# Norm sums taken in the row passes, squares on ScalarE, late features on two engines, the T1 product first, and attention memory in parts: one decoder layer on one core

## The chip, the core and the metric

The kernel runs on one core of a Trainium2 chip. The metric is the device time of the program in microseconds; it was run three times, and the number compared is the median. TensorE (PE, with its weight loads PEld) multiplies, VectorE (DVE), ScalarE (ACT) and GpSimd (POOL) work on rows in SBUF, and SyncE (SP) issues nearly all DMA transfers from one queue in program order.

## The reference

One layer of a decoder for 1024 prompt rows and 8 x 8 = 64 sample rows, width 1024. A mixer (one half sliding-window attention, the other a spatial gating unit) and a feed-forward part, each with an adaptive modulation ahead and a norm behind:

```python
h = layer_norm(x) * (1 + scale1) + shift1
q, k, v, zu, zv = split(h @ w_in)
A = attention(rotary(q), rotary(k), v, sinks)      # 8 heads, 2 key heads, window 128
B = gelu(zu) * (tril(w_s) @ layer_norm(gelu(zv)) + b_s)
x = layer_norm(ALPHA * x + gate1 * concat(A, B) @ w_o, ln1_g, ln1_b)
h = layer_norm(x) * (1 + scale2) + shift2
x = layer_norm(ALPHA * x + gate2 * (silu(h @ w_gate) * (h @ w_up)) @ w_down, ln2_g, ln2_b)
...
var = mean((xf - mu)**2);  y = (xf - mu) * rsqrt(var + LN_EPS) * gain + bias
```

shift, scale and gate come from silu(c) @ w_ada + b_ada. All is float32. The feed-forward width is 2816. The rolled key and value windows and the normalised v rows are outputs too.

## The kernel before

Every matrix product is made from fp32 numbers split into a high part that TensorE takes (ScalarE copies it) and a low rest (VectorE subtracts); three products (high-high, high-low, low-high) are summed in PSUM. A weight unit is loaded by SP, split by `load_unit` (L104 ScalarE, L105 VectorE) or `w_split` (L956, L957), and used. The order on each engine is set by a scheduler that runs a timeline model over the program as it is written; a pool's buffer (and the memory under a pool that was closed) can be written only when its last reader is done, and the scheduler puts the waits in. PSUM has four tags, a to d, of two banks each.

The stages, with their time in the profiled run:

- **Conditioning, first projections and the gating unit** (0 to about 172 us). x is normalised in six tiles that use the memory `xb`; features go to XA and XB (three column chunks of 384, 384 and 320). Later in the stage `xb` holds the rotary tables rc and rs, the sample keys and values KC and VC, the masks, the cleared sample queries QZ and an output buffer o2s. `L414` is VectorE's pass that ends the gating unit, `L408` its products.
- **Attention** (to about 350). `project` (L496) multiplies one 128-row weight unit with the features; `rotate` shuffles the result (L505, VectorE) into `sh`, copies it (L506, ScalarE) into `z`, and rotates on POOL. Keys (units[0]) come in three chunks c, then values (units[1]) with a copy `v32`, then queries. `attend` makes scores (masked by L596), softmax (L614), the transposes of the weights (L643) and the products with the values (L651), and writes into one tile `stash` of 4 x 1024 columns. At the end `split_attention` (L449, L450) splits the stash, tile by tile, into the memory of the features.
- **Output projection and first norm** (350 to about 450). `load_wo` splits eight weight units; four go to a pool `w3`, in the memory that the attention's pools leave. `out_group(2)` multiplies tiles 6, 7 and 8 (L212), `out_tile` the tiles 0 to 5. `merge_tile` scales the sums by the gate (L838, one per half); `norm_tile` adds x, takes the statistics by `ln_stats` (two bn_stats L115, one aggregation, one add on VectorE, a power on POOL L121), applies gain and bias (L855 and the pass behind it), stores the row, takes the statistics again and normalises on ScalarE (L134). Tiles 6 and 7 (`PRE`) were multiplied in part before, and add on POOL. `ffn_features` transposes the normed tiles (L880), modulates them on ScalarE (L901), and stores every block of features to DRAM (`h_d`); prompt tiles of the first 512 places also stay in XA, split.
- **Feed-forward, gate and up** (450 to 960). The products over pairs of 128-row blocks are made by a seven-product scheme over quarters of the features: B11 and B21 (first 512 places) lie in SBUF, T1 to T4 and B22 are sums and differences of quarters read back from `h_d` into `hb` (L1089, `part`), combined on VectorE (L961) and split. `gu_head(0)` and `gu_head(1)` work with B11 and B21 alone (L967, sample part L973); `gu_p5` takes T1, `gu_p6` T2, `gu_p3` B22, `gu_p7` T3, `gu_p4` T4. `gated` stores the result to `g_d`; `copied` is the tile j.
- **Down projection and last norm** (960 to the end).

The places on which the two weight passes of a pair's head, the reads of `h_d` and the writes of `h_d` meet are the SP queue and VectorE: both run in their program's order, whoever waits first. The code of the T stage is written so: heads 0 and 1; then T1 from eight reads, one statement for `gu_s1` of both pairs (L1100), then B22 and T2 to T4 from sixteen reads, then `gu_22` and `sample_down`, and only then `gu_p5` of both pairs.

## Time and profile before

| | us |
|---|---|
| three runs | 1190.87, 1191.7, 1192.7; median 1191.7 |
| the profiled execution | 1190.98, its span 1189.2 |
| mean granted TensorE clock in it | 0.979 |
| POOL busy | 171.1 (14%) |
| HBM read, written | 149.43 MB, 55.44 MB |

Busy times are sums over the span, in which stages with different limits follow one another. The rows of the slices give busy tenths and the clock that TensorE was granted; a slice below 9 on PE is a place where it waited. The profile's share of the chain that ended last is 76% PE and 10% DVE. A group of the profile (line, engine, operation, out<-in) has its busy time, the mean of one instruction in ns, and the idle time ahead of it with its releaser.

### The profile page before, as it was taken

Reading aid. Unit: us, or ns where it says so; the run is one execution under the profiler, and the core shown is the slowest. Engines: PE = TensorE matmul, PEld = TensorE weight load, DVE = VectorE, ACT = ScalarE, POOL = GpSimd, SP = SyncE. Lnnn points to the kernel's source line nnn. Section 1 sums busy time; section 2 is a strip of 40 time slices with the busy share of each in tenths; the row PEclk is TensorE's granted clock in tenths of the full one; section 3 lists DMA queues with packets and bytes.
Section 4 is the critical chain, followed back from the end, with each engine's and each line's share of the span. In section 5 each row is a group of like instructions: output and inputs, shape, how many; then the busy total and the mean of one; then the engine's idle time right before and its main releaser. Section 6 shows DMA issues by size and latency. Waiting matters only on the chain.

```text
span 1189.2 us, 16244 instructions
## 1 busy us (share of the span) xinstructions
PE 1126.9 (95%) x5845; PEld 914.7 (77%) x5845; DVE 801.2 (67%) x1460; ACT 505.3 (42%) x920; POOL 171.1 (14%) x173
## 2 busy tenths in 40 slices
PE   4999998999979999799999999999999999999997
PEld 2676688887758877477888888888888888788885
DVE  4434355898776979568487467467467565879786
ACT  3553124675761255545444434434433454343200
POOL 2212434654135111000000000000000000000021
PEclk9999998999989999799999999999999999999999
DMA  9935344122353424554545515515514488957951
GB/s 330 296 109 188 96 148 154 56 76 94 107 194 119 152 100 168 181 175 139 202 161 195 203 47 193 204 54 186 203 52 170 151 313 290 336 193 258 325 204 71
DMA packets 96352, 204.96 MB, mean 172 GB/s; under 512 B 10304, under 2 KB 32704, under 8 KB 96256
## 3 DMA queue, kind: packets, MB, share of 16 engines
q1 hardware_dynamic: 96272, 203.92, 49.6%
q8 instruction: 46, 0.75, 0.3%
q14 instruction: 34, 0.28, 0.1%
HBM read 149.43 MB, written 55.44 MB: 172 GB/s over the span
## 4 chain that ended last, share of the span: by engine, by line
PE 76%; DVE 10%; DMA 7%; ACT 3%; issue 2%; SPq 1%; POOL 1%; DVEq 0%; ACTq 0%; POOLq 0%
PE ps_a L967 17%; PE ps_b L967 13%; PE ps_a L212 11%; PE ps_b L212 4%; PE ps_c L973 3%; PE ps_a L1243 3%; PE ps_b L1243 3%; PE ps_c L1243 3%; PE ps_d L1243 3%; DMA g<-g_d 2%; PE ps_a L496 2%; DMA rwd<-in_w_down 1%; PE ps_d L364 1%; DVE s L614 1%; DVE bn L115 1%
## 5 line engine op out<-in xcount | busy, mean ns | idle before, releaser
L967 PE MATMUL ps_a<-H,wgu 128*128 128x512 f32 x560 | 160.1, 390 | 1.3 <-ACT wgu L956 1.3
L967 PEld LDWEIGHTS ps_a<-H,wgu 128*128 128x128 f32 x560 | 105.1, 188 | 23.7 <-ACT wgu L956 1.7
L957 DVE TENSOR_TENSOR wgu<-rawgu,wgu 128x1024 fp32r<-128x1024 f32 x79 | 96.2, 1220 | 33.1 <-ACT wgu L956 33.0
L1280 POOL TENSOR_TENSOR rstd<-ve,neghalf 128x1 f32<-128x1 f32 (+1 forms) x9 | 13.6, 1513 | 695.1 <-DVE ve L1278 695.1
L212 PE MATMUL ps_a<-unit,XA 128*128 128x512 f32 x384 | 103.9, 413 | 6.5 <-ACT unit L104 4.7
L956 ACT ACTIVATE wgu<-rawgu 128x1024 fp32r<-128x1024 f32 x79 | 82.0, 1055 | 58.4 <-PE ps_a L967 48.0
L967 PE MATMUL ps_b<-H,wgu 128*128 128x512 f32 x320 | 104.1, 390 | 0.0
L967 PE MATMUL ps_b<-XA,wgu 128*128 128x512 f32 x344 | 96.6, 396 | 0.0
L212 PEld LDWEIGHTS ps_a<-unit,XA 128*128 128x128 f32 x384 | 73.2, 196 | 28.0 <-ACT unit L104 4.9
L873 DVE TENSOR_TENSOR tpo<-tpr,tpo 128x512 fp32r<-128x512 f32 x77 | 50.9, 686 | 60.6 <-ACT tpo L872 60.6
L967 PEld LDWEIGHTS ps_b<-XA,wgu 128*128 128x128 f32 x344 | 65.0, 191 | 13.2
L872 ACT ACTIVATE tpo<-tpr 128x512 fp32r<-128x512 f32 x77 | 45.1, 625 | 66.8 <-DMA tpr<-in_w_down 32.5
L967 PEld LDWEIGHTS ps_b<-H,wgu 128*128 128x128 f32 x320 | 60.0, 188 | 12.7 <-ACT H L872 0.5
L967 PE MATMUL ps_a<-XB,wgu 128*128 128x512 f32 x160 | 62.4, 390 | 0.0
L961 DVE TENSOR_TENSOR rawgu<-rawgu 128x1024 f32<-128x1024 f32 x44 | 53.3, 1211 | 12.4 <-DMA rawgu<-in_w_gu 12.4
L1243 PE MATMUL ps_a<-opnd 128*128 128x512 f32 x198 | 57.9, 391 | 3.2 <-ACT opnd L1220 3.2
L967 PE MATMUL ps_a<-XA,wgu 128*128 128x512 f32 x240 | 59.8, 392 | 0.0
L1243 PE MATMUL ps_b<-opnd 128*128 128x512 f32 x198 | 57.6, 389 | 0.0
L1243 PE MATMUL ps_c<-opnd 128*128 128x512 f32 x198 | 57.4, 389 | 0.0
L1243 PE MATMUL ps_d<-opnd 128*128 128x512 f32 x198 | 57.2, 389 | 0.0
L496 PE MATMUL ps_a<-XA,unit 128*128 128x384 f32 (+1 forms) x264 | 51.5, 342 | 4.8 <-ACT z L506 3.3
L967 PEld LDWEIGHTS ps_a<-XA,wgu 128*128 128x128 f32 x240 | 44.3, 188 | 8.8
(361 smaller groups left out, 2355.9 us busy)
## 6 DMA issues: line engine op xcount, KB each, us to landing
rawgu<-in_w_gu SPq DMA_DIRECT2D x44, 512.0 KB
t_d<-tpo SPq DMA_DIRECT2D x44, 512.0 KB
opnd<-t_d SPq DMA_DIRECT2D x33, 512.0 KB
tpr<-in_w_down SPq DMA_DIRECT2D x22, 512.0 KB
g<-g_d SPq DMA_DIRECT2D x44, 256.0 KB
u<-in_w_ada SPq DMA_DIRECT2D x32, 256.0 KB
raw<-in_w_ada SPq DMA_DIRECT2D x16, 512.0 KB
raw<-in_w_ada SPq DMA_DIRECT2D x32, 256.0 KB
```

What stands on the lines that cost most here:

```text
L115: nc.vector.bn_stats(out=bn[:rows, h, :], in_=src[:, 512 * h : 512 * (h + 1)])
L212: mm(out=pt, lhsT=X[c][:, xp, k, off : off + P], rhs=rhs_of(units, k, wp), start=st and q == 0, stop=sp and q == 2)
L496: mm(out=pt[:, :n], lhsT=w[:, wp, k * P : (k + 1) * P], rhs=X[c][:, xp, k, :], start=(k == 0 and q == 0), stop=(k == KD - 1 and q == 2))
L872: nc.scalar.activation(out=hi, in_=src, func=AF.Copy)
L873: nc.vector.tensor_tensor(out=lo, in0=src, in1=hi.bitcast(F32), op=ALU.subtract)
L956: nc.scalar.activation(out=w[:, 0], in_=r, func=AF.Copy)
L957: nc.vector.tensor_tensor(out=w[:, 1], in0=r, in1=w[:, 0].bitcast(F32), op=ALU.subtract)
L961: nc.vector.tensor_tensor(out=out, in0=in0, in1=in1, op=op)
L967: mm(out=banks[m], lhsT=w[:, wp, m, k * P : (k + 1) * P], rhs=b[xp][:, k, :], start=first and k == 0 and q == 0, stop=last and k == 3 and ...
L973: mm(out=pt[:, 256 * half : 256 * half + 256], lhsT=XF[:, k0 + k, :], rhs=w[:, wp, :, k * P : (k + 1) * P], start=first and k == 0 and wp ...
L1243: mm(out=banks[tb], lhsT=st[sp][:, tb * P : (tb + 1) * P], rhs=mv[wp], start=first and q == 0, stop=last and q == 2, skip_group_check=True)
L1280: nc.gpsimd.tensor_tensor(out=rstd[:rows], in0=ve[:rows], in1=neghalf[:rows], op=ALU.pow)
```

## The change

It has five parts.

1. **Early key temporaries.** `xb` is cut into `xb` (5 x 1024 columns) and a pool `xc` of its own that holds QZ and o2s. The shuffle and copy of key chunks 0 and 1 (`sh`, `z`) no longer take buffers of `rt`, but the memory of KC and VC, and the first two `v32` that of o2s and QZ. So the loads of KC and VC move from the gating stage behind the key chunks, and the clearing of QZ (POOL) behind the value chunks. `sh` gets a pool of its own.
2. **Attention memory in parts.** `stash` becomes four tiles in four pools (two query tiles each), and the pool of the output weights, `w3`, four pools of one buffer.
3. **Norm statistics.** In `norm_tile` the bn_stats go. The row sum comes out of the passes that run anyway (`accum_out` of the add, and of the gain and bias pass), a small VectorE pass makes the mean, a ScalarE pass squares the centred row and sums it (its row output goes to `xt`, which so is held longer), another small one makes the variance, and POOL takes the power. PRE tiles add on VectorE instead of POOL. `h32` has 4 buffers instead of 6.
4. **Late features.** The features of the last tiles (tiles 3, 4 and 5, as `normed[6:8]` and `normed[8:9]`; they are places 5 to 7 and so lie in the second 512) are made by `late_features`: four transposes into one bank, the modulation of every other block on VectorE instead of ScalarE, and one DMA for a bank: 6 writes instead of 16.
5. **T1 product in front.** `gu_head(1)` loads two weight blocks instead of four; behind T1 come `gu_s1(0)` and at once the T1 product of pair 0, then the other two blocks of pair 1, `gu_s1(1)`, `gu_22` and `sample_down` of both pairs, and behind them B22 and T2 to T4. The T1 product of pair 1 stays where it was. `sample_down` transposes into its own sample bank instead of bank b.

The core of the diff:

```diff
+    xc = xcp.tile([P, D], F32, name="xc")
+    xb = xbp.tile([P, 5 * D], F32, name="xb")
...
+    QZ, o2s = xc[:, 0:512], xc[:, 512:1024]
+    early = [t[:, o : o + 384] for t in (KC, VC) for o in (0, 512)] + [o2s[:, 0:384], QZ[:, 0:384]]
...
-        nc.sync.dma_start(out=KC, in_=kc_t)
-        nc.sync.dma_start(out=VC, in_=vc_t)
...
-    stash = stp.tile([P, 4, SEQ], F32, name="stash")
+    for n in (3, 0, 1, 2):
+        stp = st_ctx.enter_context(tc.tile_pool(name=f"stash{n}", bufs=1, side="right", reuse_waits="tile"))
+        stash[n] = stp.tile([P, 4, 2 * P], F32, name=f"stash{n}")
...
-            sh = rt.tile([P, 384], F32, tag="sh", name="sh")
-            z = rt.tile([P, 384], F32, tag="z", name="z")
+            sh, z = own or [q.tile([P, 384], F32, tag=g, name=g) for q, g in ((shp, "sh"), (rt, "z"))]
...
-            z = rotate(project(units[0], c, "aac"[c]), c)
+            z = rotate(project(units[0], c, "aac"[c]), c, early[2 * c : 2 * c + 2] if c < 2 else None)
...
+        nc.sync.dma_start(out=KC, in_=kc_t)
+        nc.sync.dma_start(out=VC, in_=vc_t)
...
-            v32 = rt.tile([P, 384], F32, tag="z", name="v32")
+            v32 = early[4 + c] if c < 2 else rt.tile([P, 384], F32, tag="z", name="v32")
...
+        nc.gpsimd.memset(QZ, 0.0)
...
-        w3 = w3_ctx.enter_context(tc.tile_pool(name="w3", bufs=4, side="right", reuse_waits="tile"))
+        w3 = [
+            w3_ctx.enter_context(tc.tile_pool(name=f"w3{n}", bufs=1, side="right", reuse_waits="tile"))
+            for n in range(4)
+        ]
...
         def norm_tile(i, r, xt):
...
+            def spread(o):
+                nc.vector.tensor_scalar(
+                    out=st[:, o + 1 : o + 2], in0=st[:, o : o + 1], scalar1=-1.0 / D, scalar2=None, op0=ALU.mult
+                )
+                nc.scalar.activation(
+                    out=xt[:rows], in_=rr, func=AF.Square, bias=st[:, o + 1 : o + 2], accum_out=st[:, o + 2 : o + 3]
+                )
...
+                nc.gpsimd.tensor_tensor(out=rstd[:rows], in0=st[:, o + 3 : o + 4], in1=neghalf[:rows], op=ALU.pow)
+                return st[:, o + 1 : o + 2], rstd[:rows]
...
-            mv, rstd = ln_stats(rr, D, rows)
             nc.vector.scalar_tensor_tensor(
-                out=rr, in0=rr, scalar=mv[:rows, 0:1], in1=lg[:rows], op0=ALU.subtract, op1=ALU.mult
+                out=rr, in0=xt[:rows], scalar=1.0 if i in PRE else ALPHA, in1=rr, op0=ALU.mult, op1=ALU.add,
+                accum_out=st[:, 0:1],
             )
+            nm, rstd = spread(0)
+            nc.vector.scalar_tensor_tensor(out=rr, in0=rr, scalar=nm, in1=lg[:rows], op0=ALU.add, op1=ALU.mult)
             nc.vector.scalar_tensor_tensor(
-                out=rr, in0=rr, scalar=rstd[:rows, 0:1], in1=lb[:rows], op0=ALU.mult, op1=ALU.add
+                out=rr, in0=rr, scalar=rstd, in1=lb[:rows], op0=ALU.mult, op1=ALU.add, accum_out=st[:, 4:5]
             )
...
+        def late_features(xn):
+            w = P * len(xn)
+            kb = 512 // w
+            o = P * PLACE[xn[0][0]]
+            for k0 in range(0, KD, kb):
...
+                for kk in range(kb):
+                    cs = slice(w * kk, w * kk + w)
+                    sc_, sh_ = scale_of(mod2, k0 + kk)[:, 0:1], shift_of(mod2, k0 + kk)[:, 0:1]
+                    if kk % 2:
+                        nc.vector.tensor_scalar(
+                            out=h[:, cs], in0=pt[:, cs], scalar1=sc_, scalar2=sh_, op0=ALU.mult, op1=ALU.add
+                        )
+                    else:
+                        nc.scalar.activation(out=h[:, cs], in_=pt[:, cs], func=AF.Identity, scale=sc_, bias=sh_)
+                nc.sync.dma_start(
+                    out=h_d[k0 : k0 + kb, :, o : o + w].rearrange("k p t -> p k t"),
+                    in_=h.rearrange("p (k t) -> p k t", k=kb),
+                )
...
-        rs = w_raws(p)
+        rs = w_raws(p, range(2) if p == 1 else range(4))
...
-        pt = bank("b" if p < 2 else "d")
+        pt = sp if p < 2 else bank("d")
...
-        w1 = [gu_s1(p, rs, sp) for p, (rs, sa, sp) in enumerate(heads)]
+        w1 = [gu_s1(0, heads[0][0], heads[0][2])]
+        p5 = [gu_p5(0, heads[0][0], w1[0], "b")]
+        heads[1][0].extend(w_raws(1, range(2, 4)))
+        w1.append(gu_s1(1, heads[1][0], heads[1][2]))
+        for p, (rs, sa, sp) in enumerate(heads):
+            gu_22(p, rs, sp)
+            sample_down(p, sp)
...
-        p5 = [gu_p5(p, rs, w1[p], "bd"[p]) for p, rs, sa in two]
+        p5.append(gu_p5(1, heads[1][0], w1[1], "d"))
```

Where instructions stand is decided by the scheduler, so the two programs' order is shown at three places. First VectorE, where the gating unit ends and the keys begin; before (L414 is the gating pass, L505 the keys' shuffle out of PSUM, L105 a weight split):

```order
L394 TENSOR_TENSOR gvt<-g_1412,gvt 128x512
L414 SCALAR_TENSOR_TENSOR u_1_124<-ps_b,bst,u_1_124 128x4x64 x6
L105 TENSOR_TENSOR unit<-raw,unit 128x1024
L414 SCALAR_TENSOR_TENSOR u_1_124<-ps_b,bst,u_1_124 128x4x64 x2
L505 STREAM_SHUFFLE sh<-ps_a 128x384 x2
```

The same place on VectorE in the changed program (its lines are 2 to 3 higher; xb is the memory of KC and VC):

```order
L508 STREAM_SHUFFLE xb<-ps_a 128x384
L396 TENSOR_TENSOR gvt<-g_1414,gvt 128x512
L508 STREAM_SHUFFLE xb<-ps_a 128x384
L416 SCALAR_TENSOR_TENSOR u_1_128<-ps_b,bst,u_1_128 128x4x64 x4
L508 STREAM_SHUFFLE sh<-ps_c 128x320
L105 TENSOR_TENSOR unit<-raw,unit 128x1024
L416 SCALAR_TENSOR_TENSOR u_1_128<-ps_b,bst,u_1_128 128x4x64 x4
```

The two shuffles of bank a moved ahead of the eight last gating passes. The second place is TensorE at the end of the attention, before (L643 transposes, L651 products with the values, L212 the output projection):

```order
L643 MATMUL ps_c<-ident,s 128x128 x4
L651 MATMUL ps_d<-pT,VS 128x256 x5
L643 MATMUL ps_c<-ident,s 128x128 x4
L651 MATMUL ps_d<-pT,VS 128x256 x3
L643 MATMUL ps_c<-ident,s 128x128 x4
L651 MATMUL ps_d<-pT,VS 128x256 x8
L212 MATMUL ps_a<-unit,XA 128x512 x4
L212 MATMUL ps_b<-unit,XA 128x512 x4
```

And in the changed program (L649 and L657 are the transposes and the products with the values there):

```order
L649 MATMUL ps_c<-ident,s 128x128 x4
L212 MATMUL ps_a<-unit,XA 128x512 x2
L212 MATMUL ps_b<-unit,XA 128x512 x2
L657 MATMUL ps_d<-pT,VS 128x256
L212 MATMUL ps_a<-unit,XA 128x512 x10
L212 MATMUL ps_b<-unit,XA 128x512 x10
L657 MATMUL ps_d<-pT,VS 128x256 x4
L212 MATMUL ps_a<-unit,XA 128x512 x4
L212 MATMUL ps_b<-unit,XA 128x512
L649 MATMUL ps_c<-ident,s 128x128
L657 MATMUL ps_d<-pT,VS 128x256 x3
L649 MATMUL ps_c<-ident,s 128x128 x7
```

The first output products now stand between the last attention steps instead of behind them. The third place is the SP queue, where the last features are written and the reads for T1 begin, before (L906 writes features, L950 loads gate and up weights, L979 stores a gated tile):

```order
L906 DMA h_d<-h_4691 128x128
L906 DMA h_d<-h_4696 128x128
L950 DMA rawgu<-in_w_gu 128x1024 x2
L1089 DMA hb<-h_d 128x512 x6
L979 DMA g_d<-j_4891 128x512
L1089 DMA hb<-h_d 128x512 x2
```

And after (L961 writes late features, L1138 reads for the T sums, L999 loads weights, L1028 stores):

```order
L961 DMA h_d<-hl 128x2x256 x3
L1028 DMA g_d<-j_4736 128x512
L961 DMA h_d<-hl 128x2x256
L961 DMA h_d<-hl 128x4x128 x2
L1138 DMA hb<-h_d 128x512 x4
L999 DMA rawgu<-in_w_gu 128x1024 x2
L1138 DMA hb<-h_d 128x512
L1028 DMA g_d<-j_4824 128x512
L1138 DMA hb<-h_d 128x512 x7
```

Six wide writes stand for the sixteen narrow ones, the two weight loads moved from ahead of the reads to behind the first four, and no row is left between the last write and the first read.

55 lines of the change are left out of this document (30 added, 25 removed).

## The prediction

> **What bounds the kernel now.** I read the page's head first, then its slices, then three stretches where TensorE is not full, and there the waits and the timeline.
>
> ```profile
> span 1189.2 us, 16244 instructions
> PE 1126.9 (95%) x5845; PEld 914.7 (77%) x5845; DVE 801.2 (67%) x1460; ACT 505.3 (42%) x920; POOL 171.1 (14%) x173
> PE   4999998999979999799999999999999999999997
> PEclk9999998999989999799999999999999999999999
> ```
>
> TensorE bounds the kernel, and it is short of work only at the start, in slices 6, 11 and 16 (counted from 0, 29.7 us each) and at the end. From slice 17 to 38 it stays full, and the change hardly touches what runs there. So only these stretches can pay:
>
> ```profile
> 172.00:205.00 33.00, 28.21 (x163) 27.59 (x163) 17.57 (x36) 12.96 (x27) 10.56 (x11) 0.90 0.44 153
> 325.00:360.00 35.00, 25.63 (x189) 19.26 (x188) 24.02 (x62) 21.86 (x52) 14.62 (x11) 0.85 0.55 185
> 447.70:542.30 94.60, 81.50 (x342) 62.12 (x341) 67.85 (x104) 51.11 (x87) 4.82 (x5) 0.87 0.49 165
> ...
> PE ps_d L973 <- DVE wgu L957: 4.4, 3, 1.9
> PE ps_a L496 <- ACT z L506: 3.3, 1, 3.3
> ```
>
> The columns of a window are its length, busy time of PE, weight loads, DVE, ACT and POOL, the granted clock, and DMA. TensorE idles 4.8, 9.4 and 13.1 us in them, and runs at 0.85 to 0.90 of its clock: each gap is paid again in slow products after it. The last two rows are TensorE's waits (product and releaser: idle us, times, longest): few single waits are long, so the idle time is looked for row by row. A timeline row gives start, duration, engine, line and operation, and in brackets the wait and its releaser.
>
> **Part 1, early key temporaries.** The keys' second block was multiplied by 171.8, but its two readers come late, since their outputs lie in memory that the stage before still uses. Bank a (two buffers) stays full, and the values' first block waits for it.
>
> ```profile
> 167.51 4.32 PE L496 MATMUL ps_a<-XB,unit 128*128 128x384 f32 x24
> 179.93 0.58 DVE L505 STREAM_SHUFFLE sh<-ps_a 128x384 f32<-128x384 f32 x1
> 181.14 7.27 PE L496 MATMUL ps_a<-XA,unit 128*128 128x384 f32 x24 [3.27 <-ACT z L506]
> 188.25 4.33 PE L496 MATMUL ps_a<-XB,unit 128*128 128x384 f32 x24
> 194.10 2.61 PE L496 MATMUL ps_a<-XA,unit 128*128 128x320 f32 x16 [1.52 <-ACT v L548]
> ```
>
> It costs 3.27 idle, 7.27 - 4.33 = 2.94 of slow products, and 1.52 more: 7.7 us. The change puts these temporaries where the sample keys and values (KC, VC) would lie, and the order has the shuffles ahead of L414, so the bank is free about 174, before TensorE asks for it (181.14 - 3.27 = 177.9). What is late next is the query rotation on POOL; two more query blocks (the 4.33 above and a narrower one, some 8 us) lie between query block 0 and the first scores and cover it. KC and VC are loaded behind it: their issue waits on the SP queue for the key splits, with conditioning weights behind it, and nobody reads them before 320; I cost that at nothing (a late weight load could cost a wait of 1 to 3 us). The clearing of QZ joins POOL's queue between query rotations, about one 0.5 to 1 us pass. I take **7.5** of the 7.7. The lower end is 0: behind it DVE is nearly full, and could swallow the head start:
>
> ```profile
> 240.00:260.00 20.00, 19.52 (x140) 19.14 (x139) 19.73 (x67) 14.80 (x41) 11.53 (x13) 1.00 0.15 48
> ```
>
> **Part 2, attention memory in parts.** The first output weights (L104) wait until the last split of the one large stash is over, though the masks were last read at 334:
>
> ```profile
> 333.98 0.48 DVE L596 CUSTOM_DVE_ANT_0 s<-ps_b,xb,nsnk 128x256 f32<-128x256 f32 x1
> 350.32 2.00 ACT L104 ACTIVATE unit<-raw 128x1024 fp32r<-128x1024 f32 x2 [0.84 <-DVE XB L450]
> 351.43 2.08 PE L212 MATMUL ps_a<-unit,XA 128*128 128x512 f32 x4 [4.70 <-ACT unit L104]
> 353.30 1.67 PE L212 MATMUL ps_b<-unit,XA 128*128 128x512 f32 x4
> ...
> 335.00:340.00 5.00, 3.62 (x36) 2.53 (x36) 3.70 (x13) 2.90 (x9) 0.71 (x1) 0.75 0.85 205
> 340.00:345.00 5.00, 4.36 (x26) 3.46 (x26) 4.94 (x10) 4.27 (x8) 2.41 (x2) 0.91 0.47 178
> 345.00:350.00 5.00, 0.98 (x7) 0.58 (x5) 4.55 (x9) 3.20 (x6) 0.00 (x0) 0.77 0.37 105
> 350.00:355.00 5.00, 3.57 (x9) 2.61 (x10) 2.64 (x3) 2.95 (x3) 1.17 (x1) 0.54 0.99 383
> ```
>
> Idle: 1.38 + 0.64 + 4.02 + 1.43 = 7.5 us. The eight first products take 3.75 where 8 x 0.227 (24 in 5.44, below) is 1.8, so 1.9 more: 9.4. With parts, two weight splits stand right behind the last masked scores, and 36 of the 48 products of tiles 6 and 7 lie between the last attention steps. Their 8.2 us (x 0.227) fill the gaps; what is late next is the attention chain itself, which three weight splits on DVE (3 x 1.22) now delay, against DVE idle of 1.3 and 0.1 in the first two windows; some 1 us remains. I take **8.5**; the ends are 0 (another tile in the same memory still holds the weights) and 9.4.
>
> **Part 3, norms, late features, T1.** From the last output product (447.7) to 542.3 the same products stand in both programs: 240 of 512 columns, 64 of 256, 42 or less of 128.
>
> ```profile
> 466.88 7.08 PE ps_b L967 x24
> 542.30 5.68 PE ps_a L967 x24
> 547.99 5.44 PE ps_c L967 x24
> ...
> 449.41 1.59 PE L973 MATMUL ps_d<-wgu,XF 128*128 128x256 f32 x12
> 450.12 0.67 DVE L838 TENSOR_TENSOR r<-ps_b,g1p 128x512 f32<-128x512 f32 x1
> 475.29 0.55 POOL L121 TENSOR_TENSOR rstd<-ve,neghalf 128x1 f32<-128x1 f32 x1 [3.21 <-DVE ve L119]
> 477.26 1.23 ACT L134 ACTIVATE r<-r,nb,rstd 128x1024 f32<-128x1024 f32 x1
> 478.40 5.10 ACT L901 ACTIVATE h<-ps_c,mod 128x256 f32<-128x256 f32 x10
> 479.00 4.00 PE L880 MATMUL ps_c<-ident,r 128*128 128x128 f32 x8 [0.89 <-ACT h L901]
> 484.95 9.77 SPq L1089 DMA_DIRECT2D hb<-h_d  x6
> 491.34 0.69 DVE L961 TENSOR_TENSOR hb<-hb 128x512 f32<-128x512 f32 x1
> 501.97 0.50 PE L967 MATMUL ps_d<-H,wgu 128*128 128x512 f32 x1 [1.31 <-DVE ts L961]
> 505.41 5.93 SPq L1089 DMA_DIRECT2D hb<-h_d  x4
> ...
> L115 DVE BATCH_NORM_STATS2 bn<-r 128x6 f32<-128x512 f32 x32 | 20.0, 678 | 0.1
> L855 DVE SCALAR_TENSOR_TENSOR r<-r,mv,lg 128x1024 f32<-128x1024 f32 x8 | 10.2, 1278 | 0.0
> L134 ACT ACTIVATE r<-r,nb,rstd 128x1024 f32<-128x1024 f32 x8 | 9.9, 1242 | 16.1 <-DVE nb L131 16.1
> L957 DVE TENSOR_TENSOR wgu<-rawgu,wgu 128x1024 fp32r<-128x1024 f32 x5 | 6.1, 1221 | 1.2 <-ACT wgu L956 1.1
> ```
>
> At full speed they need 240 x 0.227 + 64 x 0.13 + about 4 = 67 us, so some 28 of 94.6 are lost. The last tile's sums leave PSUM at 450.8, and its transposes start at 479.0, since DVE is full.
>
> Removed: four L115 per tile, 2.7 us of DVE. Added: two squaring passes on ACT, at L134's 1.24 and a short read-out each. The nine tiles' 2.8 us each (25 us) lie beside products that fill TensorE; if ACT had no room, they would come out again in part. The sum in the pass that already runs is not in this trace: between 0 and another 1.28; I take 0 to 0.1, as a pass with two sources reads at one rate here.
>
> Walking DVE's new order from the last L838: about 6.2 us of other tiles' and weights' passes (1.28, 1.22, 2 x 1.2, 3 x 0.4 and small ones), the tile's first pass 1.2, two weight splits and a sum 3.65 (the square lies beside them), two norm passes 2.6, a sum 1.2, three splits 1.3: 16.2. Then square 1.4, POOL 0.6, normalization 1.24 and hand-overs of about 1.5: 21, so transposes near 472 instead of 479. The features that took ten ACT passes from 478.4 are shared by two engines and two writes. Behind the first half go head 1's 24 products (5.44, perhaps 7), so the second half is written near 481 and the T1 reads issue there, not at 484.95 behind two weight loads. By the issue row the before needed 3.5 to 6.4 us to the first use at 491.34 (the row's six issues begin at 484.95); T1's first operand stands near 488, and its product there instead of 501.97. Its last operands are paced by DMA and two weight loads ahead of them on SP; near 495 the T2 to T4 reads start, which stand at 505.41 now. That chain took 30 us, is not changed, and now ends the stage: with the second T1 product beside it, TensorE reaches the row of 542.30 some **12** us sooner. Ends: 0, if the last tile is normalized no sooner, and 20, if only 8 of 28 stay lost.
>
> **Sum.** 7.5 + 8.5 + 12 = 28. The profiled execution took 1191.0 in all (1189.2 and 1.8 around it), 0.7 below the median shown; 1191.0 - 28 = **1163 us**.
>
> **Rivals.**
> - **T1 first only moves the wait.** The T2 to T4 chain waits for the same two DVE and DMA queues as before, so only about 4 of the 12 remain: 1171. For it: that chain is behind T1 on the queues. Against: its first reads can issue some 10 us sooner.
> - **The attention pieces do not carry.** DVE at 19.73 of 20 swallows part 1, or the weights still wait as before: 1163 + 8 to 16 = 1171 to 1179. Against: DVE has 15.4 of 33 idle at the entrance.
> - **The summing pass costs double.** At 2 x 1.28 for 18 passes DVE gets 23 us, about what 36 L115 (24 us) give up. The middle stays hidden under TensorE, but the last two tiles are some 5 us later: 1168. [...]
> - **Slower: DVE waits in line for the square and for POOL.** Each statistic now crosses DVE, ACT, DVE, POOL, DVE. If nothing lay between, a tile would hold DVE 9 us of work and 2 x 3 to 4.5 of waits (square 1.24, POOL 0.55, hand-overs, at most the 3.21 of POOL's row), 15 to 18, where TensorE brings a tile every 11 us (48 x 0.227). Above 11 it decides: six tiles lose 4 to 7 each, up to 42, and with 28 - 12 gained the time is about 1215. Against: the order has other tiles' passes between nearly all of these pairs.
>
> **How the numbers follow.** Forecast 0.58, T1 0.16, attention 0.10, double sum 0.08, slower 0.08. Range: the ends of the terms do not fall together; 1150 is 28 and the upper ends of parts 2 and 3 plus a little on the clock, 1181 leaves 10 gained. By 0.2% (about 2 us, what a measurement of this kernel tells from no change) faster has 0.90 (of the attention and T1 cases 0.02 go to same), same 0.02, slower 0.08.
>
> **What would show it.** Right: no wait of the values' products for z; L212 between the last attention products, window 345 to 355 full at clock 1; transposes of the last tile some 21 us after its last sums; T1's product 13 us after that. Wrong: an accumulating pass near 2.5 us, DVE idle on ACT between 360 and 447 with TensorE below 20 of 20, or the T2 to T4 products still ending 90 us after the last output product.

## The result and the profile after

| | before | changed |
|---|---|---|
| median of six runs each (us) | 1192.2 (1190.87 to 1195.15) | 1183.53 (1182.93 to 1185.2) |
| ratio, with its 95% interval | 1 | 0.9928 (0.9914 to 0.9942) |
| profiled execution, its span (us) | 1190.98, 1189.2 | 1184.88, 1183.1 |

The change gains 8.7 us by the medians and 6.1 by the profiled spans. The forecast was 28, and 1183.53 lies 2.5 above the end of the range. First the slices of the changed kernel's page:

```profile
PE   4999999989989998799999999999999999999997
PEclk9999999998999999789999999999999999999999
```

Slice 6 is full now and slice 11 a little better, but slices 8 and 15 have lost work that they had, and slices 9 and 17 clock. To see what each stage gave, both traces are cut where TensorE has done the same product columns: entrance of the attention, its middle, its tail into the output projection, and the T stage. The windows of the kernel before, then of the changed one, with the columns of the prediction's windows:

```profile
176.39:223.62 47.23, 41.70 (x244) 40.61 (x243) 28.80 (x64) 22.22 (x51) 25.89 (x26) 0.93 0.32 109
223.62:314.05 90.43, 86.74 (x724) 73.68 (x723) 79.91 (x257) 62.59 (x179) 40.53 (x43) 0.98 0.29 92
314.05:371.60 57.55, 47.89 (x318) 37.80 (x317) 39.10 (x101) 32.49 (x80) 18.27 (x13) 0.91 0.46 154
447.20:561.23 114.03, 100.93 (x429) 78.26 (x428) 84.70 (x124) 59.46 (x98) 4.82 (x5) 0.90 0.50 170
```

```profile
176.81:216.21 39.40, 38.48 (x246) 37.95 (x246) 27.45 (x65) 23.94 (x57) 22.10 (x25) 1.00 0.45 158
216.21:313.02 96.81, 89.07 (x733) 75.07 (x732) 87.26 (x263) 61.50 (x176) 39.41 (x43) 0.96 0.28 91
313.02:365.50 52.48, 46.79 (x306) 36.99 (x305) 33.84 (x89) 29.81 (x73) 14.01 (x11) 0.93 0.47 159
441.96:554.31 112.35, 98.94 (x433) 78.58 (x432) 83.53 (x126) 62.77 (x103) 3.72 (x5) 0.89 0.53 180
```

The lengths differ by -7.8 at the entrance, **+6.4** in the middle, -5.1 in the tail and -1.7 in the T stage. The output projection between the last two (371.60 to 447.20, 365.50 to 441.96) is 0.9 longer, and what lies ahead and behind 1.2, which makes -6.1. The gain at the entrance came as forecast, and in these two executions most of it was handed back in the middle: TensorE idles 0.9 us instead of 5.5 at the entrance, but 7.7 instead of 3.7 in the middle. The T stage, which had the largest term, gave almost nothing; TensorE idles 13.4 us in it, where it idled 13.1. The 2.6 us between the medians' 8.7 and the profiles' 6.1 come from the two executions that were profiled: 1190.98 lies 1.2 below the median of the one kernel, 1184.88 lies 1.35 above that of the other.

**The entrance.** The changed kernel's windows over the two times that the prediction looked at:

```profile
172.00:205.00 33.00, 33.00 (x216) 32.87 (x215) 19.02 (x40) 15.97 (x32) 17.59 (x18) 1.00 0.53 185
...
240.00:260.00 20.00, 17.60 (x147) 15.52 (x145) 19.67 (x47) 12.80 (x33) 10.34 (x11) 1.00 0.09 26
```

172 to 205 is full at clock 1: no value product waits any more. But between 240 and 260, where TensorE had 19.52 of 20, it has 17.60, with VectorE as full as before (19.67): 47 passes now fill a time that 67 filled.

**The middle.** The same 36 softmax scalings stand in both middles. The groups of VectorE in that stage, first before, then changed:

```profile
L596 DVE CUSTOM_DVE_ANT_0 s<-ps_b,xb,nsnk 128x256 f32<-128x256 f32 x42 | 18.6, 474 | 0.6 <-PE ps_c L643 0.4
L614 DVE TENSOR_SCALAR s<-s,den 128x256 f32<-128x256 f32 x36 | 16.4, 509 | 0.1
```

```profile
L620 DVE TENSOR_SCALAR s<-s,den 128x256 f32<-128x256 f32 x36 | 21.5, 652 | 0.3
L602 DVE CUSTOM_DVE_ANT_0 s<-ps_b,xb,nsnk 128x256 f32<-128x256 f32 x42 | 18.6, 476 | 2.7 <-PE ps_c L649 2.5
```

The masked scores, which read PSUM, take 18.6 us in both. The scaling, which reads and writes SBUF, takes 5.1 us more for the same work. One step of each kind shows why; four scalings before (VectorE alone), then four in the changed kernel with what POOL does meanwhile:

```profile
235.25 1.13 DVE L614 TENSOR_SCALAR s<-s,den 128x256 f32<-128x256 f32 x4
```

```profile
248.25 3.49 DVE L620 TENSOR_SCALAR s<-s,den 128x256 f32<-128x256 f32 x4
248.47 1.02 POOL L109 TENSOR_TENSOR sh<-sh,xb 128x384 f32<-128x384 f32 x1
249.45 1.06 POOL L109 TENSOR_TENSOR z<-z,xb 128x384 f32<-128x384 f32 x1
250.59 1.00 POOL L109 TENSOR_TENSOR z<-z,sh 128x384 f32<-128x384 f32 x1
```

Four scalings take 1.13 us alone and 3.49 beside three passes of the query rotation: the first, begun 0.22 ahead of them, takes 0.35; the other three take 1.10 to 1.16 each and end 0.15 behind the ends of the three POOL passes (249.49, 250.51, 251.59). The four scalings ahead of the middle went the other way, from 3.96 to 2.60 us, so the whole program has 24.1 us of them instead of 20.3. Of the 40 scalings of the whole program 20 lay beside POOL before, 27 after. Why they last until POOL's passes end these rows do not show.

**The tail.** The changed kernel's timeline where its last attention products end:

```profile
353.24 2.08 PE L212 MATMUL ps_a<-unit,XA 128*128 128x512 f32 x4 [2.00 <-ACT unit L104]
355.11 1.71 PE L212 MATMUL ps_b<-unit,XA 128*128 128x512 f32 x4
```

Its windows there:

```profile
345.00:350.00 5.00, 5.00 (x31) 4.24 (x29) 2.93 (x7) 2.20 (x5) 0.00 (x0) 1.00 0.66 183
350.00:355.00 5.00, 3.00 (x13) 2.44 (x12) 4.76 (x9) 3.40 (x6) 0.00 (x0) 0.80 0.94 306
```

Output products fill 345 to 350 at full clock, where there were 0.98 of 5. But the fourth weight unit still comes only with the end of the attention: a wait of 2.0 instead of 4.7 us, with slow products behind it (the two rows, 2.08 and 1.71 us for eight) as before.

**The T stage.** The SP queue of the changed kernel from T1's reads to the last read, then T1's first product on TensorE (the first eight reads are T1's, the ninth begins at 492.17):

```profile
477.38 4.37 SPq L1138 DMA_DIRECT2D hb<-h_d  x4
...
492.17 6.89 SPq L1138 DMA_DIRECT2D hb<-h_d  x4
...
505.64 14.94 SPq L1138 DMA_DIRECT2D hb<-h_d  x9
522.84 2.31 SPq L1138 DMA_DIRECT2D hb<-h_d  x3
...
484.54 1.22 PE L1016 MATMUL ps_b<-H,wgu 128*128 128x512 f32 x2 [4.18 <-ACT H L896]
```

And the same queue before, with the first and the last of the sixteen reads for B22 and T2 to T4:

```profile
503.68 7.67 SPq L1089 DMA_DIRECT2D hb<-h_d  x5
...
524.37 9.29 SPq L1089 DMA_DIRECT2D hb<-h_d  x7
```

Counted from the start of the stage (447.20 and 441.96), T1's reads stand 35.4 behind it instead of 37.8, the first T2 to T4 read 50.2 instead of 56.5, the last one ends 83.2 behind instead of 86.5. The head start shrinks from 6.3 to 3.3 us, because the sixteen reads take 33.0 us instead of 30.0. VectorE shows what lies between (L1010 on hb is a T sum, which frees the reads' buffers; L1010 on rawgu and L1006 are weight passes):

```profile
494.56 0.68 DVE L1010 TENSOR_TENSOR hb<-hb 128x512 f32<-128x512 f32 x1
495.16 1.22 DVE L1010 TENSOR_TENSOR rawgu<-rawgu 128x1024 f32<-128x1024 f32 x1
496.30 1.22 DVE L1006 TENSOR_TENSOR wgu<-rawgu,wgu 128x1024 fp32r<-128x1024 f32 x1
...
498.64 1.21 DVE L1010 TENSOR_TENSOR rawgu<-rawgu 128x1024 f32<-128x1024 f32 x1
...
500.38 2.34 DVE L1006 TENSOR_TENSOR wgu<-rawgu,wgu 128x1024 fp32r<-128x1024 f32 x2
...
503.78 1.23 DVE L1006 TENSOR_TENSOR wgu<-rawgu,wgu 128x1024 fp32r<-128x1024 f32 x1
504.93 0.69 DVE L1010 TENSOR_TENSOR hb<-hb 128x512 f32<-128x512 f32 x1
```

Between the T sums at 494.56 and 504.93 VectorE does six weight passes, 7.2 us, and the read at 505.64 stands right behind the second of these sums. In the program before, `gu_22` and the sample parts stood behind the T sums; the change writes them ahead.

### The profile page after: what moved, and what is told of

Same layout as the page of the kernel before. It is cut to its first block, busy times and chain, and to the rows that moved or that the text cites. A ratio compares the mean times of both kernels' runs of the same rounds, so it can differ in the third digit from the quotient of the medians.

```text
span 1183.1 us, 16238 instructions
## 1 busy us (share of the span) xinstructions
PE 1122.4 (95%) x5845; PEld 912.2 (77%) x5845; DVE 790.8 (67%) x1452; ACT 521.8 (44%) x948; POOL 162.7 (14%) x171
## 4 chain that ended last, share of the span: by engine, by line
PE 62%; DMA 6%; DVE 3%; ACT 2%; issue 1%; SPq 1%; DVEq 0%; ACTq 0%
PE ps_a L1016 17%; PE ps_b L1016 14%; PE ps_a L212 4%; PE ps_b L212 3%; PE ps_c L1022 3%; PE ps_a L1295 3%; PE ps_b L1295 3%; PE ps_d L1295 3%; PE ps_c L1295 3%; DMA g<-g_d 2%; DMA rwd<-in_w_down 1%; PE ps_c L1016 1%; DMA rawgu<-in_w_gu 1%; PE ps_c L1200 1%; PE ps_d L1200 1%
## 5 line engine op out<-in xcount | busy, mean ns | idle before, releaser
L1006 DVE TENSOR_TENSOR wgu<-rawgu,wgu 128x1024 fp32r<-128x1024 f32 x79 | 96.0, 1220 | 31.6 <-ACT wgu L1005 31.1
L1016 PE MATMUL ps_b<-H,wgu 128*128 128x512 f32 x320 | 107.5, 402 | 7.0 <-ACT H L896 4.2
L1005 ACT ACTIVATE wgu<-rawgu 128x1024 fp32r<-128x1024 f32 x79 | 81.8, 1054 | 61.3 <-PE ps_a L1016 48.0
L212 PE MATMUL ps_a<-unit,XA 128*128 128x512 f32 x384 | 102.9, 410 | 3.1 <-ACT unit L104 2.0
L212 PEld LDWEIGHTS ps_a<-unit,XA 128*128 128x128 f32 x384 | 72.6, 195 | 24.2 <-issue 2.5
L1295 PE MATMUL ps_b<-opnd 128*128 128x512 f32 x198 | 57.6, 389 | 0.0
L1010 DVE TENSOR_TENSOR rawgu<-rawgu 128x1024 f32<-128x1024 f32 x44 | 53.4, 1213 | 3.3 <-DMA rawgu<-in_w_gu 3.2
L500 PE MATMUL ps_a<-XA,unit 128*128 128x384 f32 (+1 forms) x264 | 47.7, 325 | 0.0
```

The costliest lines, as they stand in the source:

```text
L212: mm(out=pt, lhsT=X[c][:, xp, k, off : off + P], rhs=rhs_of(units, k, wp), start=st and q == 0, stop=sp and q == 2)
L500: mm(out=pt[:, :n], lhsT=w[:, wp, k * P : (k + 1) * P], rhs=X[c][:, xp, k, :], start=(k == 0 and q == 0), stop=(k == KD - 1 and q == 2))
L1005: nc.scalar.activation(out=w[:, 0], in_=r, func=AF.Copy)
L1006: nc.vector.tensor_tensor(out=w[:, 1], in0=r, in1=w[:, 0].bitcast(F32), op=ALU.subtract)
L1010: nc.vector.tensor_tensor(out=out, in0=in0, in1=in1, op=op)
L1016: mm(out=banks[m], lhsT=w[:, wp, m, k * P : (k + 1) * P], rhs=b[xp][:, k, :], start=first and k == 0 and q == 0, stop=last and k == 3 and ...
```

## The experiments

Each kernel ran beside fresh runs of the kernel before on the same chip, and its ratio is to these. The changed kernel itself has 0.9928, and 0.9911 as a control on another chip, so differences of 0.002 in the ratio are not told apart. The stage lengths are those of windows cut as above, from one profiled execution each (us), and hold the slow clock as well as the idle time:

| kernel | median (runs) | ratio, 95% | entrance | middle | tail | T stage |
|---|---|---|---|---|---|---|
| before | 1192.2 (6) | 1 | 47.2 | 90.4 | 57.6 | 114.0 |
| changed | 1183.53 (6) | 0.9928 [0.9914, 0.9942] | 39.4 | 96.8 | 52.5 | 112.4 |
| changed, control | 1183.73 (6) | 0.9911 [0.9891, 0.9930] | 39.4 | 98.4 | 52.5 | 113.1 |
| part 1 and the pool of sh undone | 1191.8 (10) | 0.9971 [0.9958, 0.9984] | 50.3 | 90.4 | 57.0 | 111.9 |
| part 1 undone, pool kept | 1189.63 (9) | 0.9964 [0.9949, 0.9979] | 48.5 | 90.9 | 53.3 | 113.3 |
| part 3 undone | 1188.29 (6) | 0.9943 [0.9923, 0.9963] | 39.4 | 98.4 | 53.3 | 118.8 |
| part 4 undone | 1186.57 (6) | 0.9932 [0.9913, 0.9951] | 39.4 | 96.8 | 52.3 | 115.4 |
| part 5 undone | 1183.14 (5) | 0.9891 [0.9872, 0.9911] | 39.4 | 94.3 | 53.5 | 110.2 |
| before, with part 3's norm alone | 1194.48 (10) | 0.9995 [0.9978, 1.0013] | 47.9 | 90.3 | 59.1 | 113.1 |
| before, short POOL passes | 1187.0 (4) | 0.9937 [0.9914, 0.9960] | 47.7 | 89.1 | 56.8 | 111.0 |
| changed, short POOL passes | 1174.37 (4) | 0.9835 [0.9811, 0.9859] | 38.0 | 88.7 | 49.6 | 112.4 |
| pair 2's loads behind the reads | 1182.69 (6) | 0.9897 [0.9871, 0.9923] | 39.4 | 97.1 | 53.2 | 111.5 |
| pair 0 finished first | 1199.35 (11) | 1.0039 [1.0026, 1.0051] | 39.4 | 95.5 | 52.2 | 128.5 |
| weight passes behind the T splits | 1207.75 (4) | 1.0097 [1.0069, 1.0124] | 39.4 | 97.1 | 53.1 | 136.7 |
| T splits on POOL | 1188.74 (4) | 0.9946 [0.9926, 0.9967] | 39.4 | 95.6 | 52.3 | 117.7 |
| half the scalings on ScalarE | 1179.2 (5) | 0.9859 [0.9839, 0.9879] | 39.1 | 88.7 | 52.3 | 114.0 |
| the same, part 5 undone | 1175.26 (5) | 0.9836 [0.9815, 0.9857] | 39.1 | 88.8 | 51.9 | 110.2 |

The middle of the changed program has 7.7 to 7.8 us of idle TensorE in every run in which it was left as it is, and 94.3 to 98.4 us of length: what differs is the mean clock in it, 1.00 in the shortest (part 5 undone) and 0.95 in the longest (part 3 undone, and the control; last section).

### Which queue holds the T reads: pair 2's loads moved behind them

```diff
-            nc.sync.dma_start(out=r, in_=w_gu[p, q])
+            with tc.issue_after(reads[-1].ins) if p == 2 else ExitStack():
+                nc.sync.dma_start(out=r, in_=w_gu[p, q])
```

`reads` holds the reads of `h_d`.

> Changed kernel, with the four weight loads of pair 2 (not needed before about 546) queued on SP behind the last of the 24 reads for the T sums; in the changed kernel two of them stand ahead of 12 of these reads, and SP issues nothing from 498.7 to 501.6 and from 502 to 505. Theory 'SP stands in line': reads 13 to 24 issue 3 to 7 us sooner, the T2 to T4 products end that much sooner: 1177 to 1180. Rival 'the buffers of the reads pace it' (two per tag, emptied by VectorE in its order): the reads wait all the same, 1182 to 1184, or slower by a late load of pair 2 (a wait of 1 to 3 us about 546 to 560).

The T stage took 111.5 us, the median 1182.69. The SP queue of this run, from T1's sixth read to the last read:

```profile
486.65 38.24 SPq L1140 DMA_DIRECT2D hb<-h_d  x19
```

With no weight load between them, nineteen reads still take 38.2 us and end 83.3 behind the stage's start (441.57 in this run), against 83.2. So SP's loads are not what holds the reads; they wait for buffers, and those for VectorE (in the changed kernel 10.0 us of the waits of these reads are for its T sums), whose order is tried below.

### Undoing the parts one by one

Part 1 undone, with the pool of `sh`:

```diff
-            z = rotate(project(units[0], c, "aac"[c]), c, early[2 * c : 2 * c + 2] if c < 2 else None)
+            z = rotate(project(units[0], c, "aac"[c]), c)
...
-            sh, z = own or [q.tile([P, 384], F32, tag=g, name=g) for q, g in ((shp, "sh"), (rt, "z"))]
+            sh, z = own or [q.tile([P, 384], F32, tag=g, name=g) for q, g in ((rt, "sh"), (rt, "z"))]
```

(`v32`, the loads of KC and VC and the clearing of QZ go back too.)

> Changed kernel without the early key temporaries (part 1 undone; xb stays cut in two). The prediction's sum (7.5 us carried to the end): 1191. Theory 'given back in the attention': the 8 us won at the entrance were lost again by 313 us, so without them the time is 1183 to 1185 and the lead over the kernel before at the end of the attention's middle (about 313) is again about 1 us.

The entrance is 50.3 again, the middle 90.4: the loss in the middle belongs to part 1. The median of 1191.8 is what the forecast's 7.5 us would give, but not for that reason: the tail is 57.0 too, although part 2 is in. The timeline of this run there:

```profile
359.70 2.07 PE L212 MATMUL ps_a<-unit,XA 128*128 128x512 f32 x4 [4.70 <-ACT unit L104]
```

It is the wait of 4.70 us of the kernel before, to the digit. So two things had been undone, and the next kernel parts them: as this one, but with `sh` in its own pool.

> Part 1 undone as before, but the pool of sh stays where the change has it, so that the output weights lie over the parts of the stash as in the changed kernel. Theory 'given back in the attention': entrance 47 to 50 us long instead of 39.4, middle about 90 instead of 96.8, tail 52 to 53 as in the changed kernel: 2 to 4 us slower than it. Rival 'the tail needs part 1': the tail is 57 long again (as when the pool went too), 7 to 8 us slower. The prediction's 7.5: 7.5 slower, with a middle of unchanged length.

The tail is 53.3. So that pool, 3 KB of a partition for two buffers, is worth 3.7 us of the profiled tails, though the ratios of the two kernels (0.9971 and 0.9964) are not told apart. That it decides whether the fourth weight unit's memory is one that the last attention step still holds was argued from the program. Part 1 alone is worth 1189.63 - 1183.73 = 5.9 us by the medians of this group, between what the theory and the rival had; the two profiled executions show less, 9.1 won at the entrance and 7.6 lost in the middle. The loss is sure, what is left of the gain lies between 1.4 and 5.9.

Part 5 undone: the order of T1 before.

```diff
-        w1 = [gu_s1(0, heads[0][0], heads[0][2])]
-        p5 = [gu_p5(0, heads[0][0], w1[0], "b")]
-        heads[1][0].extend(w_raws(1, range(2, 4)))
-        w1.append(gu_s1(1, heads[1][0], heads[1][2]))
-        for p, (rs, sa, sp) in enumerate(heads):
-            gu_22(p, rs, sp)
-            sample_down(p, sp)
+        w1 = [gu_s1(p, rs, sp) for p, (rs, sa, sp) in enumerate(heads)]
...
+        for p, (rs, sa, sp) in enumerate(heads):
+            gu_22(p, rs, sp)
+            sample_down(p, sp)
+        two = [(p, rs, sa) for p, (rs, sa, sp) in enumerate(heads)]
+        p5 = [gu_p5(p, rs, w1[p], "bd"[p]) for p, rs, sa in two]
```

> Changed kernel with the T stage's order of before (part 5 undone): both gu_s1, B22 and T2 to T4, then the sample parts, then both T1 products. Theory 'T1 first only moves the wait': the T2 to T4 chain ends about where it did, 1183 to 1186 (at most the 24 products of T1, 5.4 us, come out again). The prediction's forecast: the order is worth about 8 of its 12 us, 1190 or more.

The median is that of the changed kernel, so T1 in front gains nothing here. The T stage is 110.2, shorter than in either run of it, but this goes with a better clock (0.94 against 0.89) and not with less waiting: TensorE idles 15.5 us of it, against 13.4. Whether T1 in front costs anything is not settled. The first and the last of the sixteen reads for B22 and T2 to T4 in this run:

```profile
493.46 10.12 SPq L1138 DMA_DIRECT2D hb<-h_d  x6
...
517.32 3.70 SPq L1138 DMA_DIRECT2D hb<-h_d  x4
```

Counted from the stage's start (439.19 in this run) they begin 54.3 behind it, later than the 50.2 of the changed kernel, and end 81.8 behind, sooner than its 83.2: they take 27.6 us instead of 33.0.

Part 3 undone: the norm of before, with its bn_stats and the PRE tiles' add on POOL.

```diff
-            st = e2.tile([P, 8], F32, tag="st", name="st", bufs=4)[:rows]
...
-            nm, rstd = spread(0)
...
+            if i in PRE:
+                pool_tt(rr, rr, xt[:rows], ALU.add)
...
+            mv, rstd = ln_stats(rr, D, rows)
```

> Changed kernel with the norm statistics of before (bn_stats on VectorE, part 3 undone). If the statistics on ScalarE are what brought the last tile's transposes from 479 to 474: they come about 5 us later and the time is 1186 to 1189. If ScalarE's squares only moved the load (ScalarE busy 17.4 of 20 us from 440 to 460, where TensorE now idles for weight splits): 1181 to 1184, and the idle time between 448 and 462 goes.

The T stage grows to 118.8, VectorE in it from 83.5 to 90.0 us busy. TensorE idles 19.6 us in it instead of 13.4. So the norm is worth some 6 us of the stage in this company. By the ratios it is 2 to 4 us, and their intervals overlap, so the time alone does not settle it. The next one puts the same norm alone into the kernel before (the diff above, the other way round):

> Kernel before with the norm statistics of the change alone (part 3 on its own). In the changed kernel undoing them cost 6 us of TensorE's idle time (19.6 against 13.4). If the same holds alone: stage around the T sums 108 us instead of 114, 5 to 6 us faster than before. If the statistics only pay together with the late features and the T order: within 2 us of before.

Alone it is worth nothing: ratio 0.9995, T stage 113.1 against 114.0, though VectorE has 79.7 us there instead of 84.7. Five us less of VectorE are no gain there by themselves; what the order waits for instead was not followed further.

Part 4 undone:

```diff
-        late_features(normed[6:8])
-        late_features(normed[8:9])
+        ffn_features(normed[6:8])
+        ffn_features(normed[8:9])
```

> Changed kernel with the features of tiles 3, 4 and 5 made as before (part 4 undone: 16 narrow writes, ScalarE alone). The prediction's steps: the second half is written some 4 to 6 us later, so are the T1 reads, and the time is 1187 to 1190. Theory 'the T stage is paced behind T1': VectorE's weight passes between the T1 sums and the T2 to T4 sums take up most of that, 1183 to 1186.

T stage 115.4, some 2 to 3 us longer, with 14.1 us of idle; 1186.57 lies between the two expectations, and the ratio's interval overlaps that of the changed kernel, so this one is not settled by the times. The control, the changed kernel unedited beside these:

> The changed kernel once more, unedited, as the measure for the others of these runs. Both theories: 0.9928 of the kernel before, within 0.002. Idle time of TensorE by stage as in its first profile (0.9 entrance, 7.7 attention's middle, 5.7 its tail, 13.4 around the T stage, to 0.5 each), while the stretches at half clock may fall otherwise by 3.4 us a piece.

1183.73, as the first time.

### Is it POOL that slows VectorE in the middle?

The three passes of the query rotation are cut to 48 columns, in the kernel before and in the changed one, which leaves out most of the rotation:

```diff
+            m = n if cut is None else cut
-            pool_tt(z[:, :n], z[:, :n], rc[:, t0 : t0 + n], ALU.mult)
+            pool_tt(z[:, :m], z[:, :m], rc[:, t0 : t0 + m], ALU.mult)
...
-            z = rotate(project(w, c), c)
+            z = rotate(project(w, c), c, cut=48)
```

> Kernel before, with the three POOL passes of every query rotation cut to 48 of 384 or 320 columns (most of the query rotation is left out). Theory 'POOL holds VectorE up': VectorE's passes with SBUF on both sides (L614 here, 0.34 us alone, 0.78 beside POOL) come down to a mean of 0.34 to 0.42, the attention's middle (90.4 us) gets shorter by 2 to 4. Rival 'VectorE is simply full': the mean of L614 stays at 0.55 and the middle at 90.

> Changed kernel with the same cut of the query rotation. Theory 'POOL holds VectorE up': the middle (96.8 us, 6.4 longer than before) comes down to that of the kernel before with the same cut, within 2 us, so that the changed kernel keeps its 8 us of the entrance: 13 to 17 us faster than the kernel before with the cut. Rival 'VectorE is full': the middle stays some 6 us longer than in the kernel before with the cut, and the difference stays 8 to 9.

The scalings' group in each run, first the kernel before cut so, then the changed one:

```profile
L615 DVE TENSOR_SCALAR s<-s,den 128x256 f32<-128x256 f32 x36 | 14.6, 461 | 0.1
```

```profile
L621 DVE TENSOR_SCALAR s<-s,den 128x256 f32<-128x256 f32 x36 | 12.5, 404 | 0.1
```

The scalings fall from 509 and 652 ns to 461 and 404, and the middles are 89.1 and 88.7 us, with 2.2 and 2.4 us of idle TensorE instead of 3.7 and 7.7: without the long POOL passes nothing of part 1 is handed back in the middle. The first kernel gained a little less than expected (461 ns instead of 340 to 420, 1.4 us of the middle instead of 2 to 4). The change is now worth 1187.0 - 1174.37 = 12.6 us, just under the 13 to 17 expected; in the same group the uncut pair differs by 10.7, and the intervals do not tell these two apart, so it is the stages that carry this test. But this also shortens the rotation itself, so a second test leaves POOL as it is and takes every other scaling off VectorE:

```diff
-                if j >= skip:
+                if j >= skip and j % 2:
+                    nc.scalar.activation(out=so, in_=so, func=AF.Copy, scale=den[:, j : j + 1])
+                elif j >= skip:
                     nc.vector.tensor_scalar(out=so, in0=so, scalar1=den[:, j : j + 1], scalar2=None, op0=ALU.mult)
```

> Changed kernel with every other scaling of the softmax rows (L620, VectorE with SBUF on both sides) made on ScalarE, nothing left out. Theory 'POOL holds VectorE up': about 20 of 40 passes at 0.63 us leave VectorE in the attention's middle, 8 us or more of its 96.8; ScalarE takes some 20 x 0.5 us and has 5 to 7 of 20 free; the middle comes to 89 to 93 and the time to 1176 to 1180. Rival 'ScalarE is late next': the middle stays 95 to 99, 1182 to 1186.

The groups of VectorE and ScalarE for the scaling in the whole of this run:

```profile
L622 DVE TENSOR_SCALAR s<-s,den 128x256 f32<-128x256 f32 x20 | 13.1, 685 | 0.2
L620 ACT ACTIVATE s<-s,den 128x256 f32<-128x256 f32 x20 | 9.3, 501 | 4.2 <-DVE den L617 3.0 <-DVE den L616 1.2
```

VectorE's are as slow as ever (685 ns), ScalarE's take 501 beside the same POOL passes; the middle is 88.7 with 3.0 us of idle instead of 7.7, and the ratio 0.9859 [0.9839, 0.9879] lies below both intervals of the changed kernel. The rows beside POOL and the first test show that POOL's passes stretch VectorE's, the second test that VectorE is the bound of the middle.

### What paces the T stage

First the rest of pair 0 (T2, B22, T3, T4) is made ahead of pair 1's second weight half, `gu_22` and the sample parts:

```diff
-        w1.append(gu_s1(1, heads[1][0], heads[1][2]))
-        for p, (rs, sa, sp) in enumerate(heads):
-            gu_22(p, rs, sp)
-            sample_down(p, sp)
...
+        rest(0)
+        for p, (rs, sa, sp) in enumerate(heads):
+            if p == 1:
+                w1.append(gu_s1(1, rs, sp))
+            gu_22(p, rs, sp)
+            sample_down(p, sp)
+        p5.append(gu_p5(1, heads[1][0], w1[1], "d"))
+        rest(1)
```

> Changed kernel with pair 0's T2, B22, T3 and T4 products written ahead of gu_s1 of pair 1, both gu_22 and both sample parts; pair 1 follows. Theory 'VectorE's weight passes stand between T1 and T2 to T4': 6 us of passes (five weight splits or sums of 1.22) leave the stretch 488 to 505, the 16 reads issue 5 to 8 us sooner, TensorE's idle time around the T stage falls from 13.3 to 6 to 9, and the time is 1176 to 1180. Rival 'two buffers and the landing of each read pace it, whatever VectorE does': the reads keep their 2 us apiece, 1182 to 1185.

Then the weight passes in question are held back behind the last T split of VectorE:

```diff
+        with tc.issue_after(splits[-1].ins):
+            w1.append(gu_s1(1, heads[1][0], heads[1][2]))
+            for p, (rs, sa, sp) in enumerate(heads):
+                gu_22(p, rs, sp)
+                sample_down(p, sp)
         two = [(p, rs, sa) for p, (rs, sa, sp) in enumerate(heads)]
```

> Changed kernel with gu_s1 of pair 1, both gu_22 and both sample parts held on VectorE behind the last split of the T sums. Theory 'VectorE's weight passes': the last read issues 8 to 12 us sooner than at 524.8, though TensorE then waits for the weights behind it, so the time may be as before (1180 to 1186). Rival 'reads pace it': the last read issues within 3 us of 524.8, and the time is 1186 to 1192.

Neither time came out as expected. Pair 0 first costs 16 us of the stage: TensorE then has mostly products that wait for the T operands, one after another (the longest group of waits, five for the split copies, is 11.6 us). With the weights last, the SP queue and TensorE's longest wait of that run are

```profile
494.11 23.48 SPq L1140 DMA_DIRECT2D hb<-h_d  x16
...
527.10 0.58 PE L1024 MATMUL ps_d<-wgu,XF 128*128 128x256 f32 x1 [27.80 <-ACT wgu L1007]
```

The sixteen reads take 23.5 us instead of 33.0, and the last one ends 74.5 behind the stage's start instead of 83.2: the weight passes between the T sums are what stretches them. But the products of those weights are TensorE's only other work at this time, and without them it stands for 27.8 us. So VectorE owes both at once, and neither order of the two helps. That the stage waits for the one or the other because VectorE has 83.5 us of work in its 112 is argued; the kernel before with part 3's norm had less of it and was no faster.

The next one takes the low parts of the B22 and T2 to T4 splits off VectorE and gives them to POOL:

```diff
+        def split_pool(hi, lo, src):
+            nc.scalar.activation(out=hi, in_=src, func=AF.Copy)
+            pool_tt(lo, src, hi.bitcast(F32), ALU.subtract)
```

> Changed kernel with the low parts of B22 and T2 to T4 (16 VectorE passes of 0.69 us) made by POOL, which is idle there. Theory 'VectorE's passes pace the T stage': VectorE gets 11 us, the last T read issues 3 to 8 us sooner than at 524.8 and the time is 1177 to 1181. Rival 'POOL holds VectorE up': VectorE's passes there (L1010, L1006, two SBUF sources) stretch beside POOL, by about 0.3 to 0.5 us each as L620 did, and the time is 1183 to 1190.

The T sums' group on VectorE, between the first and the last of their reads, in the changed kernel and then in this run:

```profile
L1010 DVE TENSOR_TENSOR hb<-hb 128x512 f32<-128x512 f32 x13 | 8.9, 685 | 1.8 <-DMA hb<-h_d 1.7
```

```profile
L1010 DVE TENSOR_TENSOR hb<-hb 128x512 f32<-128x512 f32 x13 | 12.2, 942 | 9.0 <-POOL XB L109 5.4 <-DMA hb<-h_d 3.5
```

The T sums read two operands in SBUF, as POOL's subtractions do; they take 942 ns instead of 685, and 5.4 us of waiting for POOL come on top. The stage is 5 us longer, as the rival had it; the intervals of the ratios overlap.

### The two findings together

Half the scalings on ScalarE, and part 5 undone (both edits as above):

> The same with the T order of before (part 5 undone). Theory 'T1 first only moves the wait': as e13, within 3 us either way. The prediction's 8 us for that order: 6 to 8 slower than e13.

1175.26, ratio 0.9836: 17 to 19 us below the kernel before and 8 below the changed kernel, the best of all that keep the whole computation. Against the former kernel (0.9859) the intervals overlap; the T stage of 110.2 against 114.0, with 14.5 us of idle against 16.1, speaks for the old order of T1 without settling it.

## Why the prediction was wrong

**Part 1 (7.5): the size was right, the cover was not.** The entrance gained 7.8 and the middle lost 6.4. What failed is how the step was closed: "The lower end is 0: behind it DVE is nearly full, and could swallow the head start". It was named as an end and not taken, and the rows that would have priced it were in the trace of before: four scalings took 1.13 us at 235.25, and 3.96 at 218.68, beside POOL. A full VectorE whose passes stretch when POOL works is a bound that moves, and a head start that shifts POOL's rotation against the softmax meets it. Why seven more scalings fall beside POOL in the new order is not settled.

**Part 2 (8.5): the mechanism was right, 5.1 came.** The failed step is "some 1 us remains": the fourth weight unit still waits 2.0 us for the last attention step, and the slow products behind that wait, 1.9 us in the old trace, remain with it. The tail of the changed kernel keeps 5.7 us of idle (52.48 - 46.79) of 9.7.

**Part 3 (12): the early links came, the last one failed.** T1's operands and its first product came as soon as forecast, within 2 to 3 us (484.54 is 42.6 behind the stage's start, the forecast's 488 is 40.8). The failed step is "That chain took 30 us, is not changed, and now ends the stage". It is the last link, and it was changed: it took 33.0, since the new order puts six weight passes of VectorE between its sums. The change as described writes these passes ahead of B22 and T2 to T4, and the forecast put them at nothing. The chain also began 6.3 earlier, not 10: the row at 505.41, taken as its start, is the second read of a burst that begins at 503.68, and the start came 2.4 later than forecast. So 3.3 us reach the last read; behind it the stage needs 29.2 us where it needed 27.6, which was not followed. That is the rival "T1 first only moves the wait", which gave 1171 by itself, and it went further than it said: 1.7 of the 12 remained, not 4 (1.1 over the prediction's own window: 94.60 before, 93.50 now). The run without part 5, with the same time, shows that the new order is no gain.

**The sum.** "The ends of the terms do not fall together" failed: the rivals on the attention and on T1 were given chances as if one excluded the other, but both came true at once, in part, in two stages where TensorE waited for VectorE. In the two profiled executions part 1 came out at 1.4 instead of 7.5 (up to 5.9 by the medians of its own test), part 2 at 5.1 instead of 8.5, part 3 at 1.7 instead of 12; with 0.9 lost in the output projection and 1.2 elsewhere that is 6.1 of 28.

**The other rivals fell.** The summing pass does not cost double. The three passes of the changed norm over the whole program, with a sum (L874 and L880) and without (L879), and a read-out of the sum:

```profile
L874 DVE SCALAR_TENSOR_TENSOR r<-xt,r 128x1024 f32<-128x1024 f32 (+1 forms) x9 | 11.9, 1327 | 3.2 <-DMA xt<-in_x 3.2
L880 DVE SCALAR_TENSOR_TENSOR r<-r,rstd,lb 128x1024 f32<-128x1024 f32 (+1 forms) x9 | 11.5, 1280 | 2.0 <-POOL rstd L871 2.0
L879 DVE SCALAR_TENSOR_TENSOR r<-r,st,lg 128x1024 f32<-128x1024 f32 (+1 forms) x9 | 11.5, 1277 | 0.0
L880 DVE DVE_READ_ACCUMULATOR r<-r,rstd,lb 128x1 f32 (+1 forms) x9 | 0.7, 81 | 0.0
```

1280 against 1277 ns, and 81 for the read-out: the value taken (0 to 0.1) holds, and the rival's 2 x 1.28 us no run shows. The mean of L874 holds one pass of 2.19 us at 368.17, which lies beside a POOL pass of 2.40 that began at 366.89; the other eight take 1.21 to 1.23. Nor does VectorE wait in line for the statistics: its idle time for POOL's power over nine tiles is 2.0 us in the row of L880 and 4.6 us ahead of a small pass behind it (L886), and the output projection is 0.9 us longer, not up to 42.

## What to carry to other kernels

Before a stage is given a head start, look at the instructions of one shape: if they take 0.34 us in one place and 1.17 in another, as the scalings did here, see what runs beside them, since a shift in time can then cost what it won. When work is moved ahead on one queue, read what it now stands in front of: a chain that "is not changed" is changed by whatever new passes stand between its links. Two shortfalls with different causes can both happen; they have to be added before the range is drawn.
